# A two-layer sequence model on one core: first weights ahead of the modulations, head decay as one minimum, schedule offsets redone

## The chip, the cores and the metric

The kernel runs on one core of a Trainium2 chip. The metric is device time in microseconds of one execution. Runs of one kernel agree within some 0.1 to 0.3%. Busy times, starts and waits come from one execution under the hardware profiler. Engines are written as in the profile: PE is the matrix engine, PEld its weight loads, DVE the vector engine, ACT the scalar engine, POOL the general engine, SP the queue that issues most DMAs.

## What is computed

Two layers over 256 context tokens and 256 latent tokens of width 1024, all in float32. Every norm is followed by a modulation, whose shift, scale and gate come from a product of SiLU(c) with a 1024 x 6144 matrix for each layer.

```python
for layer in range(DEPTH):                     # DEPTH = 2, ctx_out = layer 0 only
    m_lat = jnp.split(silu_c @ mod_w[layer] + mod_b[layer], 6)      # m_ctx likewise from c_ctx
    h_lat = modulate(rms_norm(lat, norm_mix_g[layer]), m_lat[0], m_lat[1])
    if layer % 2 == 0: y_ctx, y_lat = s5_retention_mixer(h_ctx, h_lat, ...)
    else:              y_ctx, y_lat = mlstm_mixer(h_ctx, h_lat, ...)
    lat = lat + m_lat[2] * y_lat
    h2 = modulate(rms_norm(lat, norm_mlp_g[layer]), m_lat[3], m_lat[4])
    lat = lat + m_lat[5] * (relu(h2 @ mlp_w1[layer]) ** 2 @ mlp_w2[layer])
    ...                                        # the same for ctx in layer 0
return rms_norm(lat, final_norm_g)
```

The even mixer projects the input to `u, q, k, v, g`, runs a bidirectional complex diagonal state space model (S5) on `u` and a bidirectional retention with four heads on `q, k, v`. Retention weighs a score of positions i and j with `exp((i-j) * log_gamma)` in the one direction and `exp((j-i) * log_gamma')` in the other; this factor is what `decay` builds. The odd mixer is an mLSTM.

## The kernel before

The Python code does not issue instructions in the order in which it is written. It records operations in a plan, each with its engine, its tiles and a group name (`u`, `mods`, `norm0`, `nm0`, ...; `.w` marks weight loads, `.s` streamed weights of modulations). A list scheduler (`order`, `run`, `in_order`) then fixes one program for each engine: it takes operations by a rank, with an offset of the rank for each group, and lets a group take new buffers only up to a horizon ahead of the most urgent operation, with an allowance for each group. `SHIFT` holds (offset, allowance) by group, `HORIZON` the horizon, and `AGAIN` further passes with their own tables; the best pass by the scheduler's own costs is taken. `emit` issues everything, so nearly every instruction bears line 745 of the code (746 in the changed kernel). Each engine runs its program in order, and an instruction that waits holds up all that stands behind it on that engine.

Weights come as 128x1024 tiles of 512 KB. Products are done in a split format: ACT casts a tile to its high part (`CAST w<-w`), DVE subtracts to get the low part (`TENSOR_TENSOR w<-w,w`), which is called a split below, and three matmuls (high by high, low by high, high by low) make one product. Activations are split in the same way, unit by unit (eight units `k` of 128 features, 512 tokens or twice 256).

The opening is written as follows. The input x is loaded, its squares are summed, and `rstd_of` makes the root. Eight modulations `mod_first` load 2 x 512 KB of weights each, do eight matmuls with `sc` (SiLU of c, from the small input `cc`) into a row, which ACT copies to `mrow`, and four tiny matmuls with `msel` turn it into columns. `mod_gain` and `norm_k` then give the units of the first norm (`norm0`). The four weight tiles of the first product `u` are loaded after that, then the S5 parameters are computed on DVE (`s5_parameters`, many instructions of 128x64). `plan.behind` names a DMA that all DMAs recorded after it have to follow. `LATE` lists the modulations whose weights go to tiles of the large pool `w` (10 tiles of 128x1024) instead of two halves in the pool `b` (59 tiles of 128x512).

`decay(hd, kt)` builds from the distances `dk` (128x256) the exponent `lg*max(dk,0) + lneg*min(dk,0)` with two TENSOR_SCALARs and an add, and three exponentials. It is called eight times.

Three norms stand between two dense products: `nm0` ahead of the first MLP (around 325 us in the profile), `nm` ahead of the second layer's mixer (around 700), `nm1` ahead of the last MLP (around 982). At each, PE adds up squares (`MATMUL ps<-ones,b`), DVE makes the root in nine tiny instructions on `rs`, PE broadcasts it (`MATMUL ps<-ident,rs`), DVE and ACT make the units, and the MLP's first products take the units with three weight tiles.

Of the kernel before, what the change touches and what calls it, by code (L numbers as in the profile page):

```python
# [21 lines left out]
HORIZON, ROUNDS = 73, 6  # L22
SHIFT = {"": (-41, 76), "chu00": (-8, 8), "chu01": (0, 156), "chu10": (0, -100), "chu11": (0, 27), "decay0": (0, 8),
# [41 lines left out]
)  # L65
MAGIC = 12582912.0
LIGHT = {(0, 0): range(8), (0, 1): (1, 3, 5, 6, 7), (1, 0): (1, 3, 5, 6, 7)}
LATE = (1, 3, 6)
VEC = {}
_off = 0  # L70
for _n, _w in (("modb", 96), ("nmix", 16), ("nmlp", 16), ("nfin", 8), ("bglu", 8), ("retgn", 4),
# [1174 lines left out]
def even_mixer(x):  # L1246
# [321 lines left out]
    def decay(hd, kt):  # L1568
        f, b = hd, 4 + hd
# [337 lines left out]
```

## Time and profile before

| | |
|---|---|
| runs (three) | 1183.42 us median, 1182.99 to 1184.41 |
| profiled execution | 1184.34 us, span 1182.6 us |
| granted PE clock, mean | 0.988 |
| busy in the span | PE 1133.5, PEld 963.2, DVE 832.1, ACT 553.7, POOL 30.5 us |
| DMA | 182.24 MB, mean 154 GB/s |

The span is the time from the first to the last instruction that the profiler saw. Busy time of PE counts matmuls that run one behind the other without a gap as busy. In a timeline row the first number is the start, the second the length of a group of like instructions that follow each other, `x` their count, and what stands in brackets is the engine's idle time just before and the row that ended it. In a row of a stretch (start:end, length) each engine's busy time follows with its number of instructions, then the granted PE clock, the share of the DMA engines and GB/s.

### The profile page before, as it was taken

The numbers are of one execution on the slowest core, as the hardware profiler recorded it, in microseconds if no ns is written. First come the engines' busy times: TensorE is split into PE (matmuls) and PEld (weight loads), VectorE is DVE, ScalarE is ACT, GpSimd is POOL, SyncE is SP. The second block draws the span as 40 slices with busy tenths as digits, with TensorE's granted clock in tenths as the row PEclk, the third lists the DMA queues.
The fourth block names the chain that finished last, engine by engine and source line by source line (L and its number), as shares of the span: only waits on it lengthen the run. The fifth ranks groups of instructions, "written<-read, shape, count | busy, mean of one in ns | idle before, by whom it ended". The sixth has DMA issues, their size and how long they took to land.

```text
span 1182.6 us, 18205 instructions
## 1 busy us (share of the span) xinstructions
PE 1133.5 (96%) x7104; PEld 963.2 (81%) x7104; DVE 832.1 (70%) x1635; ACT 553.7 (47%) x902; POOL 30.5 (3%) x61
## 2 busy tenths in 40 slices
PE   5799999999999999999999999999999998999996
PEld 3577786778998777887878898688788997999996
DVE  7999999658989685347543577669677656763755
ACT  4636656433363422122432346468856544543642
POOL 0000000000001010011000000000000000000000
PEclk9799999999999999999999999999999998999998
DMA  8764645315446375357352523425322353555642
GB/s 309 272 205 141 226 155 181 113 45 175 148 142 176 112 265 195 108 197 264 107 178 71 165 94 95 128 90 161 107 70 57 98 187 121 181 187 189 200 158 90
DMA packets 65750, 182.24 MB, mean 154 GB/s; under 512 B 11136, under 2 KB 17472, under 8 KB 65664
## 3 DMA queue, kind: packets, MB, share of 16 engines
q1 hardware_dynamic: 57600, 151.71, 39.4%
q0 software_dynamic: 8064, 29.36, 7.7%
q8 instruction: 56, 0.92, 0.3%
q14 instruction: 30, 0.25, 0.1%
HBM read 178.20 MB, written 2.85 MB: 153 GB/s over the span
## 4 chain that ended last, share of the span: by engine, by line
PE 72%; DVE 9%; ACT 2%; issue 1%; DMA 1%; DVEq 0%; SPq 0%; ACTq 0%
PE ps L745 72%; DVE b L745 7%; DVE w L745 1%; ACT b L745 1%; DMA b<-in_bdq 1%; DVE rs L745 0%; ACT w L745 0%; ACT L745 0%; DVE mv L745 0%; DVE sm L745 0%; DVE tz L745 0%; DVE e L745 0%; ACT tz L745 0%; DVEq L1903 0%; DVE den L745 0%
## 5 line engine op out<-in xcount | busy, mean ns | idle before, releaser
L745 PE MATMUL ps<-b,w 128*128 128x256 f32 (+1 forms) x5232 | 921.0, 335 | 6.5 <-ACT w L745 2.5
L745 PEld LDWEIGHTS ps<-b,w 128*128 128x128 f32 x5232 | 781.6, 189 | 121.3 <-issue 11.4
L745 DVE TENSOR_TENSOR w<-w,w 128x1024 fp32r<-128x1024 f32 x209 | 255.7, 1224 | 172.0 <-PE ps L745 110.7
L745 ACT CAST w<-w 128x1024 fp32r<-128x1024 f32 x209 | 218.7, 1049 | 319.1 <-PE ps L745 153.2
L745 DVE TENSOR_TENSOR b<-b,b 128x512 f32<-128x512 f32 (+4 forms) x287 | 154.5, 557 | 51.5 <-ACT b L745 45.1
L745 PE MATMUL ps<-b,b 128*128 128x256 f32 (+5 forms) x832 | 142.6, 338 | 4.0 <-ACT b L745 1.8
L745 PEld LDWEIGHTS ps<-b,b 128*128 128x128 f32 (+2 forms) x832 | 97.9, 169 | 31.3 <-issue 17.0
L745 DVE SCALAR_TENSOR_TENSOR e<-e,sc,e 128x1024 f32<-128x1024 f32 x70 | 88.0, 1280 | 7.1 <-DMA e<-in_modc 6.6
L745 ACT ACTIVATE b<-ps 128x256 f32<-128x256 f32 (+1 forms) x112 | 49.9, 459 | 72.5 <-PE ps L745 71.4
L745 ACT COPY b<-ps 128x256 f32<-128x256 f32 (+4 forms) x136 | 60.4, 463 | 37.8 <-PE ps L745 32.3
L745 ACT ACTIVATE b<-b 128x256 f32<-128x256 f32 (+1 forms) x78 | 38.6, 503 | 72.9 <-DVE b L745 65.9
L745 ACT CAST b<-b 128x256 fp32r<-128x256 f32 (+1 forms) x120 | 57.3, 497 | 27.3 <-DVE b L745 26.1
L745 DVE SCALAR_TENSOR_TENSOR b<-b,vec,b 128x512 f32<-128x512 f32 (+1 forms) x80 | 52.7, 694 | 9.4 <-ACT b L745 9.1
L745 DVE TENSOR_TENSOR b<-b 128x256 f32<-128x256 f32 (+2 forms) x95 | 44.1, 479 | 18.2 <-ACT b L745 18.1
L745 DVE SCALAR_TENSOR_TENSOR b<-ps,mc,b 128x256 f32<-128x256 f32 x72 | 32.7, 479 | 26.6 <-PE ps L745 26.3
L745 POOL DMA_DIRECT2D e<-in_modc x56 | 29.7, 531 | 646.3 <-DVE e L745 406.4
L745 ACT ACT_TABLE_LOAD x34 | 43.6, 1283 | 1.5 <-PEq L1899 0.7
L745 PE MATMUL ps<-ones,b 128*128 128x1 f32 x112 | 15.6, 258 | 15.8 <-DVE b L745 14.9
L745 DVE SCALAR_TENSOR_TENSOR b<-ps,b 128x512 f32<-128x512 f32 (+1 forms) x32 | 19.3, 621 | 16.2 <-PE ps L745 10.7
L745 PEld LDWEIGHTS ps<-ones,b 128*128 128x128 f32 x112 | 15.8, 211 | 17.4 <-DVE b L745 15.1
L745 PE MATMUL ps<-w,b 128*128 128x256 f32 x192 | 24.7, 284 | 0.2 <-DVE w L745 0.2
L745 PEld LDWEIGHTS ps<-w,b 128*128 128x128 f32 x192 | 23.4, 188 | 1.6 <-issue 1.0
(114 smaller groups left out, 504.5 us busy)
## 6 DMA issues: line engine op xcount, KB each, us to landing
w<-in_w SPq DMA_DIRECT2D x128, 512.0 KB, 4.3
e<-in_modc POOLq DMA_DIRECT2D x56, 512.0 KB, 4.4
m<-in_modc SPq DMA_DIRECT2D x24, 512.0 KB, 4.7
w<-in_evin SPq DMA_DIRECT2D x16, 512.0 KB, 5.5
w<-in_mlx SPq DMA_DIRECT2D x16, 512.0 KB, 4.5
w<-in_mlo SPq DMA_DIRECT2D x16, 512.0 KB, 3.7
w<-in_mlout SPq DMA_DIRECT2D x16, 512.0 KB, 3.9
b<-in_modw SPq DMA_DIRECT2D x20, 256.0 KB, 5.5
```

The source lines that it names most:

```text
L745: o.ins.append(getattr(engine, name)(*[f(a) for a in args], **{k: f(v) for k, v in kw.items()}))
```

## The change

1. The four weight tiles of `u` are recorded ahead of the modulations, and the modulations' loads from the second pair on (i = 1, 2, 3) have to follow the third of these four loads.
2. `LATE` is empty: all modulation weights of the opening lie in halves in the pool `b`. It is 32 loads of 256 KB now, in place of 20 of 256 KB and 6 of 512 KB.
3. `decay` makes the exponent as `min(lg*dk, lneg*dk)`: an ACT copy with a scale gives `lneg*dk`, and one SCALAR_TENSOR_TENSOR multiplies and takes the minimum.
4. `HORIZON` goes from 73 to 110, many entries of `SHIFT` and all of `AGAIN` are replaced.

```diff
-HORIZON, ROUNDS = 73, 6
+HORIZON, ROUNDS = 110, 6
-         ... "nm": (25, 54), "nm0": (-25, -30), "nm1": (68, -98), "norm0": (-66, 226), ...
+         ... "nm": (0, 227), "nm0": (-25, -30), "nm1": (68, -98), "norm0": (-72, 226), ...
-         (125.3, {"": (3.9, 135), "chu00": (0, 65), ...
+         (42.5, {"": (-9, 130), "chu00": (0, 10), ...
-LATE = (1, 3, 6)
+LATE = ()
@@ even_mixer
         x.ss_add(ss, k)
+    with x.plan.group("u"):
+        w_u = [x.weight(I["evin"][i]) for i in range(4)]
+    hold = [o for o in x.plan.ops if o.dma][-2]
     r = x.rstd_of(ss, 0, 1.0 / 1024)
     h = ([], [])
     for i in range(4):
+        x.plan.behind = hold if i else None
         x.plan.run_in("mods", x.mod_first, 4 + i)
         x.plan.run_in("mods", x.mod_first, i)
         x.mod_gain(0, 0, True, 2 * i, 2)
         for k in (2 * i, 2 * i + 1):
             x.plan.run_in("norm0", x.norm_k, h, r, k, 0, 0)
-    with x.plan.group("u"):
-        w_u = [x.weight(I["evin"][i]) for i in range(4)]
     x.plan.behind = [o for o in x.plan.ops if o.dma][-4]
@@ decay
-        ts(e, dk, 0.0, MAX, lg[:, f:f + 1], MUL)
-        ts(c2, dk, 0.0, MIN, lneg[:, b:b + 1], MUL)
-        tt(e, e, c2, ADD)
+        act(c2, dk, AF.Copy, scale=lneg[:, b:b + 1])
+        stt(e, dk, lg[:, f:f + 1], c2, MUL, MIN)
```

The tables change the order of the whole program. Where the prediction speaks of it, the engines' programs read as follows. In a row stands the line, the operation, the tile written and the tiles read (name, buffer or record numbers) and the shape.

DVE in the opening, before; `vec` holds the S5 constants, `lgs` and the `b` tiles of 128x64 their intermediate values, `sc` is the input of the modulations:

```order
L745 SCALAR_TENSOR_TENSOR lgs_153<-vec_115 128x8
L745 TENSOR_SCALAR b_44_160<-vec_115 128x64
L745 TENSOR_TENSOR b_46_171<-vec_115 128x64
L745 TENSOR_SCALAR b_44_160<-b_44_160 128x64
L745 TENSOR_TENSOR b_46_171<-vec_115 128x64
L745 TENSOR_SCALAR b_44_160<-b_44_160 128x64
L745 TENSOR_TENSOR b_46_171<-b_46_171 128x64
L745 SCALAR_TENSOR_TENSOR b_44_160<-b_44_160 128x64
L745 RECIPROCAL b_46_171<-b_46_171 128x64
L745 SCALAR_TENSOR_TENSOR b_44_160<-b_44_160 128x64
L745 TENSOR_TENSOR sc_81<-sc_81,cc_119 128x8x2
```

In the changed order two pieces of DVE's program, the first with the second and the third of the four splits of `u` (w_58, w_61), the second with the multiplication for `sc`:

```order
L746 SCALAR_TENSOR_TENSOR b_53_213<-b_53_213 128x64
L746 SCALAR_TENSOR_TENSOR rs_52_209<-rs_52_209 128x4
L746 TENSOR_TENSOR w_58_238<-w_39_148,w_56_223 128x1024
L746 SCALAR_TENSOR_TENSOR b_53_213<-b_53_213 128x64 x2
L746 TENSOR_SCALAR b_53_213<-b_53_213 128x64
L746 TENSOR_TENSOR w_61_247<-w_41_153,w_59_240 128x1024
```

```order
L746 SCALAR_TENSOR_TENSOR b_73_300<-b_73_300 128x64
L746 TENSOR_TENSOR b_73_300<-b_73_300 128x64 x2
L746 TENSOR_TENSOR pw_23_111<-b_78_318,b_77_314 128x64
L746 TENSOR_TENSOR b_75_309<-b_75_309,b_44_159 128x64
L746 TENSOR_TENSOR b_73_300<-b_73_300 128x64
L746 TENSOR_TENSOR b_81_331<-pw_23_111 128x128
L746 TENSOR_TENSOR sc_73<-sc_73,cc_215 128x8x2
L746 TENSOR_TENSOR b_77_314<-pw_21_107,pw_23_111 128x64
```

The multiplication that makes `sc` was the 34th row of DVE's program and is the 115th; the splits of `u` and the S5 parameters (down to the powers `pw`) now stand ahead of it.

PE at the norm `nm0`, before, from a modulation (`pick`) on: triples with tiles w_653/w_699 and then w_700/w_704 of the first MLP, one after the other for one unit (b_714, b_718):

```order
L745 MATMUL ps_716_3424<-e_638_2920,pick_87 32x256 x4
L745 MATMUL ps_716_3424<-e_636_2911,pick_87 32x256 x4
L745 MATMUL ps_720_3441<-b_714_3420,w_653_2991 128x256
L745 MATMUL ps_720_3441<-b_714_3420,w_699_3291 128x256
L745 MATMUL ps_720_3441<-b_718_3436,w_653_2991 128x256
L745 MATMUL ps_723_3449<-ones_75,b_678_3124 128x1
L745 MATMUL ps_723_3449<-ones_75,b_702_3319 128x1
L745 MATMUL ps_723_3449<-ones_75,b_678_3124 128x1
L745 MATMUL ps_723_3449<-ones_75,b_702_3319 128x1
L745 MATMUL ps_729_3464<-b_714_3420,w_700_3303 128x256
L745 MATMUL ps_729_3464<-b_714_3420,w_704_3348 128x256
L745 MATMUL ps_729_3464<-b_718_3436,w_700_3303 128x256
```

In the changed order one tile (w_708/w_717) takes all units first:

```order
L746 MATMUL ps_698_3206<-b_681_3075,w_707_3294 128x256
L746 MATMUL ps_672_3037<-ident_401,mrow_678_3062 128x128 x2
L746 MATMUL ps_729_3453<-b_722_3437,w_708_3321 128x256
L746 MATMUL ps_729_3453<-b_722_3437,w_717_3414 128x256
L746 MATMUL ps_729_3453<-b_726_3447,w_708_3321 128x256
L746 MATMUL ps_729_3453<-b_730_3457,w_708_3321 128x256
L746 MATMUL ps_729_3453<-b_730_3457,w_717_3414 128x256
L746 MATMUL ps_729_3453<-b_735_3467,w_708_3321 128x256
L746 MATMUL ps_729_3453<-b_727_3449,w_708_3321 128x256
L746 MATMUL ps_729_3453<-b_727_3449,w_717_3414 128x256
L746 MATMUL ps_729_3453<-b_733_3463,w_708_3321 128x256
L746 MATMUL ps_729_3453<-b_737_3471,w_708_3321 128x256
```

DVE there, before, from the last add ahead of the norm's first product (`gm`) to the second of the tiles' splits (w_722):

```order
L745 TENSOR_TENSOR b_678_3124<-b_678_3124,b_702_3319 128x256
L745 SCALAR_TENSOR_TENSOR b_712_3416<-b_529_2403,gm_522_2373,ps_711_3404 128x256
L745 TENSOR_TENSOR b_713_3418<-b_531_2407,ps_711_3404 128x256
L745 SCALAR_TENSOR_TENSOR b_715_3422<-b_537_2436,gm_522_2373,ps_711_3404 128x256
L745 SCALAR_TENSOR_TENSOR b_547_2471<-ps_690_3198,mc_81_325,b_547_2471 128x256
L745 SCALAR_TENSOR_TENSOR b_718_3436<-b_712_3416,mc_81_325,b_714_3420 128x256
L745 TENSOR_TENSOR b_719_3439<-b_534_2425,ps_711_3404 128x256
L745 TENSOR_TENSOR w_722_3447<-w_705_3350,w_717_3433 128x1024
```

In the changed order, the end of the first stream's units and the two splits that follow (w_751, w_753):

```order
L746 SCALAR_TENSOR_TENSOR b_740_3483<-b_731_3459,mc_123_493,b_734_3465 128x256
L746 TENSOR_TENSOR b_742_3487<-b_732_3461,b_737_3471 128x256
L746 TENSOR_TENSOR b_743_3489<-b_581_2638,ps_719_3420 128x256
L746 SCALAR_TENSOR_TENSOR b_581_2638<-ps_698_3206,mc_123_493,b_581_2638 128x256
L746 TENSOR_TENSOR b_747_3504<-b_739_3478,b_744_3491 128x256
L746 TENSOR_TENSOR b_748_3506<-b_741_3485,b_745_3497 128x256
L746 TENSOR_TENSOR b_689_3143<-b_689_3143,b_711_3356 128x256
L746 TENSOR_TENSOR mc_123_493<-ps_672_3037,vec_119 128x16
L746 TENSOR_TENSOR b_750_3518<-b_746_3502,b_749_3508 128x256
L746 TENSOR_TENSOR w_751_3521<-w_688_3141,w_718_3417 128x1024
L746 TENSOR_TENSOR w_753_3531<-w_673_3046,w_714_3387 128x1024
L746 TENSOR_SCALAR rs_755_3540<-ps_752_3526 128x2
```

The splits stand behind the whole first stream instead of among its first units.

DVE ahead of the norm `nm1`, before; w_1688 and w_1693 are splits of the last MLP's tiles, b_1655 the sum of squares, `rs` the root:

```order
L745 TENSOR_TENSOR w_1684_8991<-w_1669_8862,w_1678_8930 128x1024
L745 TENSOR_TENSOR w_1685_8993<-w_1670_8865,w_1681_8970 128x1024
L745 SCALAR_TENSOR_TENSOR b_1169_6006<-ps_1667_8844,mc_871_4216,b_1169_6006 128x256
L745 TENSOR_TENSOR b_1655_8751<-b_1655_8751,b_1687_9013 128x256
L745 TENSOR_TENSOR w_1688_9034<-w_1676_8925,w_1682_8987 128x1024
L745 SCALAR_TENSOR_TENSOR b_1224_6338<-ps_1674_8907,mc_871_4216,b_1224_6338 128x256
L745 SCALAR_TENSOR_TENSOR b_1224_6338<-ps_1623_8506,mc_871_4216,b_1224_6338 128x256
L745 TENSOR_TENSOR w_1693_9046<-w_1683_8989,w_1689_9036 128x1024
L745 TENSOR_TENSOR b_1655_8751<-b_1655_8751,b_1692_9044 128x256
L745 TENSOR_SCALAR rs_1697_9058<-ps_1696_9053 128x2
```

In the changed order:

```order
L746 TENSOR_TENSOR b_1649_8661<-b_1649_8661,b_1692_9024 128x256
L746 SCALAR_TENSOR_TENSOR b_1222_6317<-ps_1676_8878,mc_961_4833,b_1222_6317 128x256
L746 SCALAR_TENSOR_TENSOR b_1222_6317<-ps_1668_8806,mc_961_4833,b_1222_6317 128x256
L746 TENSOR_TENSOR b_1649_8661<-b_1649_8661,b_1694_9039 128x256
L746 TENSOR_SCALAR rs_1697_9050<-ps_1696_9045 128x2
L746 TENSOR_SCALAR rs_1697_9050<-rs_1697_9050 128x2
L746 TENSOR_TENSOR rs_1697_9050<-rs_1697_9050 128x2 x2
L746 SCALAR_TENSOR_TENSOR rs_1697_9050<-rs_1697_9050 128x2 x2
L746 TENSOR_TENSOR rs_1697_9050<-rs_1697_9050 128x2
L746 SCALAR_TENSOR_TENSOR rs_1697_9050<-rs_1697_9050 128x2 x2
L746 TENSOR_TENSOR w_1699_9063<-w_1678_8896,w_1689_8984 128x1024
L746 SCALAR_TENSOR_TENSOR b_1701_9067<-b_1127_5707,gm_1353_6996,ps_1698_9060 128x256
```

A split (w_1699) stands right behind the root, and the other two (w_1725, w_1729) stand behind nearly all units:

```order
L746 SCALAR_TENSOR_TENSOR b_1720_9113<-b_1715_9100,mc_961_4833,b_1717_9104 128x256
L746 SCALAR_TENSOR_TENSOR b_1722_9120<-b_1716_9102,mc_961_4833,b_1719_9111 128x256
L746 SCALAR_TENSOR_TENSOR b_1723_9122<-b_1718_9109,mc_961_4833,b_1721_9118 128x256
L746 SCALAR_TENSOR_TENSOR b_1724_9127<-b_1222_6317,gm_1353_6996,ps_1698_9060 128x256
L746 TENSOR_TENSOR w_1725_9132<-w_1685_8946,w_1702_9069 128x1024
L746 SCALAR_TENSOR_TENSOR b_1727_9139<-b_1724_9127,mc_961_4833,b_1726_9134 128x256
L746 TENSOR_TENSOR w_1729_9145<-w_1680_8901,w_1700_9065 128x1024
```

No split is left between the last residual products and the sum of squares.

More of the change, by code (lines that the diff above doesn't have):

```diff
@@ L21 @@
 CAPS = {"b": 59, "w": 10, "e": 5, "m": 2, "ps": 8, "mrow": 2, "rs": 3, "tz": 2, "mv": 2, "mv1": 2, "den": 2}
-HORIZON, ROUNDS = 73, 6
-SHIFT = {"": (-41, 76), "chu00": (-8, 8), "chu01": (0, 156), "chu10": (0, -100), "chu11": (0, 27), "decay0": (0, 8),
[18 rows of a table removed]
-AGAIN = (
[5 rows of a table removed]
-         268), "gat1.w": (111.2, 353), "glu": (-3.9, 304), "glu.w": (-20.4, 128), "gt": (-3, 368), "gt.w": (-2.4,
[16 rows of a table removed]
+HORIZON, ROUNDS = 110, 6
+SHIFT = {"": (-41, 76), "chu00": (-8, 8), "chu01": (0, 162), "chu10": (0, -100), "chu11": (0, 27), "decay0": (0, 8),
[19 rows of a table added]
+AGAIN = (
[22 rows of a table added]
 )
```

80 rows, old and new, of tables (AGAIN, SHIFT) are left out of this document.

## Prediction

> **What bounds the kernel now.** I read the page first, then the engines' busy time by stretches, then TensorE's (PE) row of the timeline, where idle time stands in brackets behind the row that ended it, and last VectorE's (DVE) row at the places where PE waits.
>
> ```profile
> span 1182.6 us, 18205 instructions
> PE 1133.5 (96%) x7104; PEld 963.2 (81%) x7104; DVE 832.1 (70%) x1635; ACT 553.7 (47%) x902; POOL 30.5 (3%) x61
> PE 72%; DVE 9%; ACT 2%; issue 1%; DMA 1%; DVEq 0%; SPq 0%; ACTq 0%
> ```
>
> The span is 1182.6 us in an execution of 1184.34, which is 0.92 above the median of 1183.42. PE is busy for 96%, so over the whole there are some 49 us to lose or win; the 9% of DVE in the chain that ended last shows who holds them. The stretches say where:
>
> ```profile
> core 0: us, PE busy (x) PEld busy (x) DVE busy (x) ACT busy (x) POOL busy (x), PEclk, DMA share, GB/s
> 30.00:50.00 20.00, 13.04 (x101) 8.48 (x94) 20.00 (x84) 12.03 (x26) 0.00 (x0) 0.70 1.01 390
> 50.00:72.00 22.00, 21.47 (x88) 16.65 (x87) 22.00 (x56) 10.95 (x18) 0.00 (x0) 0.96 0.15 42
> 12.00:220.00 208.00, 192.08 (x1383) 144.41 (x1384) 201.97 (x541) 115.44 (x220) 1.21 (x2) 0.97 0.62 209
> 220.00:250.00 30.00, 30.00 (x215) 24.24 (x214) 13.57 (x38) 10.14 (x19) 0.53 (x1) 1.00 0.25 76
> 345.00:600.00 255.00, 254.78 (x1144) 204.15 (x1143) 159.66 (x184) 80.63 (x105) 21.10 (x40) 1.00 0.55 181
> 705.00:930.00 225.00, 221.65 (x1246) 184.51 (x1246) 163.80 (x372) 147.87 (x247) 0.00 (x0) 1.00 0.33 98
> ```
>
> From 12 to 220 us DVE is busy 202.0 of 208 us: there DVE is the bound, and PE has 15.9 us of idle time. From 220 us on PE is the bound (30.00 of 30, 254.78 of 255), but for short stops where a norm stands between two products. So a DVE instruction that is saved or pushed back counts in the first stretch, later only at those stops, and whatever PE loses is not won back after 220 us. Rows of PE, DVE and the DMA issues in the opening:
>
> ```profile
> 16.18 1.94 PE L745 MATMUL ps<-b,sc 128*32 128x256 f32 x16 [0.19 <-DVE lgs L745]
> 41.47 1.01 PE L745 MATMUL ps<-msel,mrow 128*128 128x2 f32 x4 [4.16 <-ACT mrow L745]
> 46.24 10.62 PE L745 MATMUL ps<-b,w 128*128 128x512 f32 x34
> 57.39 2.97 PE L745 MATMUL ps<-b,w 128*128 128x512 f32 x11 [0.53 <-DVE w L745]
> 12.35 0.19 DVE L745 TENSOR_SCALAR b<-vec 128x64 f32<-128x64 f32 x1
> 13.76 0.16 DVE L745 TENSOR_TENSOR sc<-sc,cc 128x16 f32<-128x16 f32 x1
> 21.65 3.08 DVE L745 TENSOR_TENSOR b<-b,ps 128x512 f32<-128x512 f32 x5
> 17.36 7.48 SPq L745 DMA_DIRECT2D b<-in_modw  x12
> 33.61 0.33 SPq L745 DMA_DIRECT2D w<-in_modw  x1
> ```
>
> The first modulation runs at 16.18 us, the last one late (its row is waited for until 41.47), the first product `u` starts at 46.24. The transfers' issues run at 7.48/12 = 0.62 us for each 256 KB.
>
> **The decays.** Each of eight drops two TENSOR_SCALARs and one TENSOR_TENSOR of 128x256 for one SCALAR_TENSOR_TENSOR, and one ACT copy comes in.
>
> ```profile
> L745 DVE TENSOR_SCALAR b<-b,lgs 128x256 f32<-128x256 f32 x16 | 5.1, 350 | 0.0
> L745 DVE TENSOR_TENSOR b<-b,b 128x256 f32<-128x256 f32 x62 | 26.0, 422 | 16.9 <-ACT b L745 16.5
> L745 DVE SCALAR_TENSOR_TENSOR b<-b,vec,b 128x256 f32<-128x256 f32 x16 | 7.1, 478 | 0.0
> L745 ACT COPY b<-ps 128x256 f32<-128x256 f32 x56 | 19.7, 374 | 7.1 <-PE ps L745 5.0 <-DVE b L745 2.0
> ```
>
> Neighbours on DVE overlap by about 0.08 us, so back to back these are 0.26, 0.34 and 0.39 us: 2 x 0.26 + 0.34 - 0.39 = 0.47 us of DVE, 3.7 for eight. The 16 TENSOR_SCALARs' 5.1 busy us are the union of the rows, so no more than 16 x 0.35 could be gained there. ACT gets 8 x 0.37 = 3.0 us, in a stretch where it is busy 115 of 208: nothing, except that each copy stands in the chain of its decay.
>
> **The opening.** The first product's four weights now come before most modulations. On the DMA queue 54 units of 256 KB (47 before) stand ahead of the last modulation's weights, with the input of the modulations (`cc`) itself moved from row 10 to row 22: 7 x 0.62 = 4.3 us later. On DVE the four splits (1.13 us each, from 328.30 to 329.43 in the rows further down) and nearly all of the S5 parameters stand ahead of the multiplication that makes `sc`, which ran at 13.76; by the rows' durations that is 16.5 us of work from 12.35 on, so PE's first modulation goes from 16.2 to about 29, and 16 of them follow at 1.0 to 1.9 us per 16 matmuls, with the last weights landing 4 to 5 us later than now. The norm's products on DVE, which began at 21.65, move to 39. I get the start of `u` at 48.5 to 49 instead of 46.24. Then `u` has all four tiles ready, but its third unit of the input comes from DVE only at about 60, since eight products of the S5 tables stand ahead of it; `u` ends at about 77.7 instead of 72.2, with 1.45 us of other matmuls pulled in. PE is then 4.0 us behind.
>
> How much of this is left at 250 us hangs on DVE, the bound. I add up DVE's durations in program order up to each place where PE takes from it, and the PE work that is left from there. The largest of these sums is 1134.6 before (second pair of heads) and 1138.5 in the changed order (the S5 outputs and first heads, at 188 us): 3.9 more, though the decays' 3.7 is in it, because more table and weight work is ahead of that place. The distance between such a sum and the real clock, DVE's waits and the gaps between its instructions, grows with time (7.8 us at 200, 9.9 at 218); the new maximum lies 30 us earlier, so it has 2 to 3 us less of it. 3.9 - 2.8 = **+1.1 us**; bounds: -3.7, if only the decays' saving arrives, and +4.0, if the whole delay of `u` stays.
>
> **The norm before the first MLP.** Rows of PE and DVE there, with the broadcast of the root at T = 325.41:
>
> ```profile
> 325.41 0.61 PE L745 MATMUL ps<-ident,rs 128*128 128x128 f32 x4
> 325.77 1.31 PE L745 MATMUL ps<-b,w 128*128 128x256 f32 x9
> 327.01 1.07 PE L745 MATMUL ps<-e,pick 128*32 128x256 f32 x16
> 329.29 4.60 PE L745 MATMUL ps<-b,w 128*128 128x256 f32 x36
> 326.06 0.48 DVE L745 SCALAR_TENSOR_TENSOR b<-b,gm,ps 128x256 f32<-128x256 f32 x1 [0.77 <-PE ps L745]
> 326.45 0.41 DVE L745 TENSOR_TENSOR b<-b,ps 128x256 f32<-128x256 f32 x1
> 326.78 0.47 DVE L745 SCALAR_TENSOR_TENSOR b<-b,gm,ps 128x256 f32<-128x256 f32 x1
> 328.30 1.22 DVE L745 TENSOR_TENSOR w<-w,w 128x1024 fp32r<-128x1024 f32 x1
> 329.43 0.47 DVE L745 SCALAR_TENSOR_TENSOR b<-b,mc,b 128x256 fp32r<-128x256 f32 x1
> ```
>
> Now PE takes three weight tiles in turn for each unit of the norm's output (36 matmuls in 4.43 us, 0.37 for three), so a unit gives it 1.1 us of work and DVE keeps up; it loses 0.4 us. In the changed order one tile is split ahead of the norm, the other two only behind all 18 norm instructions of the first stream. DVE starts them at T+0.65: 7 at 0.39 and 11 at 0.335 make 6.5 us, the last unit is there at T+7.2, the two splits at T+8.3 and T+9.4. PE has until then 1.9 us of other matmuls and eight triples of 0.37, ending at T+7.6: idle 7.6 - 1.9 - 2.95 = 2.75 us, less the 0.4 of now: **+2.4**. Bounds 0 (if ACT and DVE deliver so that PE is filled) and +4.5.
>
> **The last norm.**
>
> ```profile
> 975.79 3.47 PE L745 MATMUL ps<-b,w 128*128 128x256 f32 x28
> 981.77 1.05 PE L745 MATMUL ps<-ones,b 128*128 128x1 f32 x8 [2.52 <-DVE b L745]
> 984.65 1.22 PE L745 MATMUL ps<-ident,rs 128*128 128x128 f32 x4 [1.82 <-DVE rs L745]
> 986.99 12.15 PE L745 MATMUL ps<-b,w 128*128 128x256 f32 x87 [1.11 <-ACT b L745]
> 980.16 1.22 DVE L745 TENSOR_TENSOR w<-w,w 128x1024 fp32r<-128x1024 f32 x1
> 985.91 1.26 DVE L745 SCALAR_TENSOR_TENSOR b<-b,gm,ps 128x256 f32<-128x256 f32 x3 [1.32 <-PE ps L745]
> 980.00:984.00 4.00, 1.05 (x8) 0.97 (x8) 2.68 (x9) 1.75 (x3) 0.00 (x0) 0.94 0.82 266
> 987.00:990.00 3.00, 3.00 (x13) 2.86 (x14) 3.00 (x9) 1.94 (x5) 0.00 (x0) 0.50 0.00 0
> ```
>
> Here the split at 980.16 stands ahead of the add that the sums (981.77) wait for. In the changed order the three splits are behind the root: one right ahead of the norm's products, under the broadcast's wait (1.32 us idle before 985.91), two behind nearly all of them. The sums come 1.4 us earlier. Then DVE has 15 instructions of 0.39 from T+1.26 (T = the broadcast), the second tile's split ends at T+8.3, and 17 triples of 0.355 are left: T+14.3. Before, the 24 triples are done at T+12.7 (987 to 999.1 less 15 matmuls of another tile). +1.6 - 1.4 = +0.2, and the clock, half between 984 and 990 now, stays low some 1.2 us' worth longer since PE runs thin until T+8.3; half of that is mine: **+0.8**, bounds -1.4 and +4.
>
> The clock at the first MLP's norm I leave at full: PE is busy half of the time there, against 1.05 of 4.00 us in the row 980 to 984, after which it was 0.50. Should it fall, 3.4 us of dense matmuls run at half speed, +1.7. The Trainium skill (TensorE: Matmul & The Clock Gate, What's actually happening) lets the clock drop only after an idle window of about 3.4 us; by it nothing falls at either norm. This trace differs: the longest wait at the last norm is 2.52 us and the clock still halved, so the idle share decides here, not one long gap.
>
> The other norm (odd layer, some 3 us lost now) has less work under it but two splits right behind the first unit: 0, within 1 us. Between 705 and 930, where PE idles 3.4 us by the row and small waits of several kinds follow each other, the order is new everywhere, and I have no sign: 0, within 2.
>
> **Sum.** 1.1 + 2.4 + 0.8 = +4.3 on 1184.34 gives 1188.6 for such an execution, **1187.7** against the median.
>
> **Rivals.** *Faster:* the DVE-bound stretch shortens. It has 6.0 us of DVE idle and the 3.7 of the decays; if the early splits fill 3 of the 6 (the first product waited 0.53 us for a split at 57.39), the stretch gives -6.7, and with +3.2 at the norms the time is 1179.9. It decides from -5.6 us at 220 on (3.2 and the 2.4 that can be told from no change). For it: 202 of 208 us. Against: the larger sum at 188 us, and the first product that waits in a new place. *No change:* the decays' 3.7 arrive in full and the norms take back 3.2: 1182.9. *Slower still:* the whole 4.0 of the opening remains and the clock falls at the first MLP's norm: 4.0 + 2.4 + 1.7 + 0.8 = 8.9, 1192.3.
>
> **Numbers.** A measurement here tells 0.2%, 2.4 us. Forecast with its upper rival: 0.56 (0.42 for 1186 to 1190, 0.14 above); no change 0.20; faster 0.24. The range from 1178 to 1194 leaves out a tenth or less at either end; the forecast alone would be 1185.8 to 1190.
>
> **What would show it.** `u` should start at 48 to 49.5 and end near 77.5; PE's idle time up to 250 us should be about 1 us more than now, with DVE still busy over 95%; around 330 us PE should show seven or eight stops of 0.3 to 0.5 us with DVE as releaser; the sums of the last norm should follow the last product within 1.5 us instead of 2.5. I am wrong if `u` ends before 74, or if DVE's idle time in the opening falls by more than 2 us.

## The result and the profile after

The changed kernel takes 1204.58 us (median of four, 1203.33 to 1207.52); the kernel before took 1183.91 beside it. The ratio is 1.0183, 95% interval 1.0170 to 1.0196: about 21 us slower, where 1187.7 was forecast and the range ended at 1194. The page's head and its chain of the changed kernel:

```profile
span 1203.4 us, 18195 instructions
PE 1136.7 (94%) x7104; PEld 963.8 (80%) x7104; DVE 829.1 (69%) x1619; ACT 560.6 (47%) x912; POOL 30.4 (3%) x61
PE 71%; DVE 16%; DMA 5%; ACT 4%; issue 3%; SPq 0%; POOL 0%; DVEq 0%; ACTq 0%; POOLq 0%
```

PE does the same 7104 matmuls in nearly the same busy time, and DVE is busy 3.0 us less. Nearly all of the loss is waiting (PE's busy time grows by 3.2 us, the span by 20.8): in the chain that ended last DVE goes from 9% to 16% and DMA from 1% to 5%. Five of the six stretches that stood in the prediction, now:

```profile
30.00:50.00 20.00, 16.22 (x169) 9.94 (x169) 20.00 (x89) 9.56 (x22) 0.00 (x0) 0.84 1.00 330
50.00:72.00 22.00, 20.21 (x87) 15.49 (x88) 22.00 (x42) 11.84 (x24) 0.00 (x0) 0.83 0.30 105
12.00:220.00 208.00, 177.72 (x1409) 135.05 (x1409) 194.12 (x507) 114.10 (x222) 1.06 (x2) 0.96 0.57 189
220.00:250.00 30.00, 30.00 (x137) 24.11 (x135) 28.98 (x40) 13.77 (x22) 3.69 (x7) 1.00 0.77 269
705.00:930.00 225.00, 217.41 (x1208) 177.21 (x1208) 174.74 (x396) 152.82 (x247) 3.70 (x7) 0.99 0.37 119
```

From 12 to 220 us PE loses 14.4 us against before (177.72 for 192.08), and DVE is not fuller but emptier: 194.12 busy for 201.97. From 705 to 930 PE loses 4.2. PE's row in the opening:

```profile
30.31 6.06 PE L746 MATMUL ps<-b,sc 128*32 128x256 f32 x80 [13.56 <-DVE sc L746]
49.98 7.64 PE L746 MATMUL ps<-b,w 128*128 128x512 f32 x24
60.41 0.80 PE L746 MATMUL ps<-ident,b 128*128 128x128 f32 x4 [1.79 <-DVE b L746]
60.86 18.47 PE L746 MATMUL ps<-b,w 128*128 128x512 f32 x72
```

The modulations wait 13.56 us for `sc` and run from 30.31, `u` starts at 49.98 and ends at 79.2 (72.2 before). One execution is not exact here: in the profiles of e3 and h1 (below), which run the program of the kernel before up to this place, `u` starts at 43.21 and 44.51 instead of 46.24.

To place the loss I matched the two traces matmul by matmul and took, at the same amount of PE work done, start time plus PE work still to come. How much later the changed kernel stands against the kernel before, worked out from one profile of each; beside it the same for two kernels of the experiments:

| PE work done, us | place | after: starts at, behind by | g4 behind by | g6 behind by |
|---|---|---|---|---|
| 30 | end of `u` | 75, 5.7 | 1.4 | 3.6 |
| 60 | S5 tables | 107, 4.6 | 1.4 | 2.3 |
| 80 | S5 tables | 132, 9.4 | 1.4 | 6.8 |
| 160 | heads | 227, 13.5 | 1.7 | 10.7 |
| 260 | output projection | 329, 13.0 | 1.8 | 10.0 |
| 300 | behind `nm0` | 372, 15.8 | 1.7 | 12.9 |
| 620 | end of the first MLP | 693, 14.5 | 1.8 | 11.6 |
| 740 | odd mixer | 827, 21.8 | 2.9 | 17.1 |
| 900 | ahead of `nm1` | 996, 21.6 | 2.8 | 16.9 |
| 1060 | last MLP | 1163, 21.3 | 4.0 | 16.6 |

Four pieces: `u` (5.7 here), some 7 us from there to the output projection (5.7 to 13.0), 2.8 at `nm0`, 7 in the odd mixer; the stretches between take back about 2.

The piece at `u` scatters with PE's granted clock. In the eight profiles with this opening (after, g5, g6, g8 to g12) it is 2.6 to 5.9, on the mean 4.1: 2.6 to 2.8 where the clock of 50 to 72 us is 0.94 to 0.96 (g5, g8, g9), 3.6 to 5.1 where it is 0.91 to 0.87 (g6, g10, g12), 5.7 and 5.9 where it is 0.83 and 0.84 (after, g11).

The rows at 107, 132 and 227 us don't place the second piece more closely, since the two orders take matmuls of different kinds first there. PE's idle time by stretches does so roughly. Before:

```profile
72.00:120.00 48.00, 46.75 (x379) 36.45 (x379) 46.35 (x84) 26.13 (x51) 0.00 (x0) 1.00 0.63 202
120.00:190.00 70.00, 67.35 (x581) 53.13 (x580) 68.91 (x160) 42.50 (x84) 0.68 (x1) 1.00 0.61 202
190.00:220.00 30.00, 27.90 (x147) 19.16 (x147) 28.37 (x73) 17.73 (x35) 0.54 (x1) 1.00 0.47 150
```

and after:

```profile
72.00:120.00 48.00, 44.85 (x373) 36.39 (x372) 42.16 (x82) 26.95 (x51) 0.00 (x0) 1.00 0.64 191
120.00:190.00 70.00, 66.47 (x556) 50.91 (x555) 64.96 (x139) 41.49 (x85) 0.53 (x1) 1.00 0.42 136
190.00:220.00 30.00, 26.39 (x215) 18.82 (x213) 27.14 (x56) 18.11 (x36) 0.53 (x1) 0.94 0.46 162
```

PE is idle 1.9 us more from 72 to 120 us, 0.9 more from 120 to 190 and 1.5 more from 190 to 220, where a clock of 0.94 costs another 1.8 (0.06 x 30).

### The profile page after: what moved, and what is told of

Same layout as the page of the kernel before. It is cut to its first block, busy times and chain, and to the rows that moved or that the text cites. A ratio compares the mean times of both kernels' runs of the same rounds, so it can differ in the third digit from the quotient of the medians.

```text
span 1203.4 us, 18195 instructions
## 1 busy us (share of the span) xinstructions
PE 1136.7 (94%) x7104; PEld 963.8 (80%) x7104; DVE 829.1 (69%) x1619; ACT 560.6 (47%) x912; POOL 30.4 (3%) x61
## 4 chain that ended last, share of the span: by engine, by line
PE 71%; DVE 16%; DMA 5%; ACT 4%; issue 3%; SPq 0%; POOL 0%; DVEq 0%; ACTq 0%; POOLq 0%
PE ps L746 71%; DVE b L746 12%; ACT b L746 3%; DVE w L746 2%; DMA w<-in_mlx 1%; DMA dram<-b 1%; DVE e L746 1%; ACT L746 1%; DMA e<-in_modc 1%; DMA b<-in_xT 1%; DVE rs L746 0%; DMA b<-in_modw 0%; DMA m<-in_modc 0%; DVE mv L746 0%; ACT w L746 0%
## 5 line engine op out<-in xcount | busy, mean ns | idle before, releaser
L746 DVE TENSOR_TENSOR b<-b,b 128x512 f32<-128x512 f32 (+4 forms) x287 | 152.0, 556 | 64.8 <-ACT b L746 61.2
L746 DVE TENSOR_TENSOR b<-b 128x256 f32<-128x256 f32 (+2 forms) x87 | 40.8, 483 | 13.8 <-ACT b L746 13.8
L746 DVE TENSOR_TENSOR b<-pw,b 128x512 f32<-128x512 f32 x36 | 23.7, 689 | 2.1 <-DMA dram<-b 2.0
```

The costliest lines, as they stand in the source:

```text
L746: o.ins.append(getattr(engine, name)(*[f(a) for a in args], **{k: f(v) for k, v in kw.items()}))
```

## Experiments

Names in the expectations: a number behind a letter is another experiment of this list. From f on, the scheduler is replaced by a written list of all operations and one of all buffers:

```diff
-        best = self.order(HORIZON, ROUNDS)
-        self.slot, self.n = best[3], 0
+        self.slot, self.n = {b: s for b, s in zip(self.bufs, SLOTS) if s >= 0}, 0
...
-                self.emit(best[2])
+                self.emit(ORDER)
```

### The parts of the change: e1, e2, e3

e1 is the kernel after with the offsets of the kernel before, e2 the reverse.

```diff
-HORIZON, ROUNDS = 110, 6      # e1; SHIFT and AGAIN of before as well
+HORIZON, ROUNDS = 73, 6
```

> The changed code (first weights early, all modulation weights in small buffers, new decay) under the old tables of offsets, allowances and horizon, so that only the order differs from the changed kernel. Theory A (order: DVE's work ahead of the places where PE takes from it, plus DVE's waits, sets the time at 250 us, and the new tables are what made the waits long): the sum of DVE durations and PE work left is 1139.0 us at most here, the waits come out between those of before (7.5 us at 188) and of the changed kernel (14.9), so 5 to 8 us over before in the opening and little elsewhere: 1186 to 1194 us. Rival B (the structure costs: weights of u ahead of the modulations delay every order): as slow as the changed kernel, 1200 to 1208. Rival C (structure free, tables all of it): 1180 to 1186.

> The code of before under the new tables. Theory A: the sum of DVE durations and PE work left reaches 1164 us (at the retention's values, 175 us of DVE work ahead), 29 more than before; with 8 to 15 us of DVE waits the time is 1205 to 1225. Rival B (the structure costs, tables do not): 1181 to 1190.

Measured: 1272.09 (ratio 1.0750, 1.0734 to 1.0766) and 1277.08 (1.0779, 1.0754 to 1.0804). No theory had this. A table of offsets seems to fit only the recorded program that it was made for (why, no run shows); the two halves can't be priced apart in this way.

e3 is the kernel before, in its own order, with the new decay at the place of the old one:

```diff
-V tensor_scalar, V tensor_scalar, V tensor_tensor
+A activation (copy with scale), V scalar_tensor_tensor
```

> The order of before, instruction by instruction, with each decay's two TENSOR_SCALARs and add replaced where they stood by an ACT copy with a scale and one SCALAR_TENSOR_TENSOR with a minimum. It measures the decay alone. Theory A (DVE is the bound to 220 us): 0.47 us of DVE saved eight times, of which that ahead of the deciding place counts: 1180 to 1182, -2 to -3.7 us. Rival (the copies lengthen the chains through ACT, or PE hides it): 1183 to 1185.

Measured: 1183.37, ratio 0.9999 (0.9989 to 1.0008). The stretch 120 to 220 us in the kernel before (behind the length PE, PEld, DVE busy):

```profile
120.00:220.00 100.00, 95.25 (x727) 72.29 (x726) 97.28 (x231) 60.23 (x119) 1.21 (x2) 1.00 0.57 187
```

and in e3:

```profile
120.00:220.00 100.00, 94.93 (x717) 71.11 (x715) 93.53 (x214) 62.20 (x124) 1.21 (x2) 1.00 0.56 183
```

DVE is relieved of 3.75 us, as was worked out, in a stretch where it was busy 97%; PE's time does not move. The saved time came back as waiting. This was the first sign that a busy DVE is not the bound.

### Order and buffers: f1 to f4, g4

f1 takes the order of before up to the last matmul of `u` and the order of after from there, f2 the reverse, f3 the order of after to some 280 us and then that of before. f4 runs the changed operations throughout in the order of before.

> The changed code with a fixed order: up to the last matmul of the first product u, the instructions stand in the order of the kernel before (its late first weights included); all the rest stands in the order of the changed kernel. Theory A (the losses of the changed order lie in several places that add up; PE's start of u is one of them, 5.5 us): 1197 to 1200 us. Rival B (the late u is what makes the later waits of DVE, on the write of u's result to memory and after, so that the opening carries most of the 13 us lost by 250 us): 1190 to 1195. Rival C (DVE's throughput absorbs the opening): 1203 to 1206.

> The mirror image: the changed kernel's order up to the last matmul of u, the order of the kernel before from there on. Theory A: 1183.6 + 5.5 = 1189. Rival B (u's delay makes later waits): 1192 to 1197. Rival C (absorbed by 250 us): 1183 to 1185.

> The changed kernel's order up to the first output product of the even mixer (about 280 us), the order of before from there on. Theory A: the opening's 12.9 us stay, the later losses (first MLP's norm +3, odd layer +8, last norm and gate 0) go: 1195 to 1198. Rival (the later losses come with the early part's transfers and buffers, not with the later order): 1202 to 1206.

> The changed code (small buffers for all modulation weights, new decay) with every instruction at the place it had before; the weights of u are loaded where they were. Theory A (structure costs nothing, the order is all): 1182 to 1185. Rival (loads into small buffers or the ACT copies cost): 1187 or more.

Measured: f1 1213.87 (1.0262), f2 1210.48 (1.0230), f3 1197.78 (1.0120, 1.0103 to 1.0136), f4 1193.07 (1.0082, 1.0059 to 1.0104). f1 and f2 are slower than either parent: behind the seam many buffers had to take other places (in f1 DVE waits 4.4 us at 85.8 for a buffer that is still being written to DRAM, and 2.9 at 92.4 for PE), so neither answers what was asked. f3, in theory A's range, puts some 14 of the 21 us ahead of 280 us, roughly, since it has a seam too; the table's 13.0 at 260 agrees. f4 came out some 10 us above the kernel before (1183.15 beside it), and 273 of its 2038 buffers lay elsewhere than there; g4 repeats it with every old buffer at its old place.

> The kernel after, its instructions in the order of the kernel before (each instruction at the place that its counterpart has there, the added splits at the place of the load they follow), and every buffer that has a counterpart in the kernel before in that counterpart's slot; only the modulation weights' halves, which are new in the small buffers, take free slots. f4 had the same order, but 273 of 2038 buffers in other slots, and took 1193.07. Theory A (the 20 us of the kernel after come from the order and the choice of buffers, not from what the change computes or loads): 1181 to 1186, ratio 0.998 to 1.002, with the first product's matmuls some 2 us earlier than in the kernel before and the DVE stretch of 12 to 220 us at 198 to 202 us busy. Then the choice of slots alone cost f4 7 to 12 us. Theory B (weights in small buffers cost by themselves, through the pool that they fill): 1190 to 1196, as f4.

Measured: 1185.29, ratio 1.0019 (1.0006 to 1.0032): theory A. The 2 us by which `u` was to be earlier did not come; in the profile, which is the slowest of g4's eight runs (1188.09), it stands 1.4 later. DVE's waits from 12 to 220 us in f4 that g4 has not (sum, times, longest):

```profile
DVE w L959 <- ACT w L959: 3.8, 1, 3.8
DVE w L959 <- issue: 2.1, 1, 2.1
```

These two rows, 5.9 us for tiles of the pool `w`, are gone in g4.

So the changed operations, small buffers and new decay included, cost 2 us (1 to 4) when they run in the old order, and the choice of buffers alone, in the same order, is worth 7.8 us (1193.07 to 1185.29). All but some 2 of the 21 us are the new order with the buffers that go with it.

### The odd mixer: g6

> The kernel after with two weight tiles of the odd layer staged in the two modulation buffers of the same size, which stand empty from early on, and their loads put on SyncE's queue where it blocked: issued near 712 us instead of 735.6. All ten weight slots are held there until 735 to 738 us, and five loads then land together at 743.0 to 750.3; ScalarE waits 3.36 us for one and 1.88 us for another with activations queued behind that PE needs. Theory A (the 8 us lost at 705 to 785 us come from weights that are late because their slots are held): 1199.5 to 1202.7, the casts' waits for loads gone or under 1 us, and the loss of 705 to 785 us at 3 to 6 us. Theory B (the stretch is held by ScalarE's and VectorE's own order, the late loads are hidden): 1203.5 to 1206. Theory C (the earlier loads delay the third gate tile's, which lands at 717.45): 1206 to 1209.

```diff
-2 tiles: pool w (10 tiles, all held), DMA behind 711.31 on SP: issued from 735.62 on
+2 tiles: pool m (2 tiles, empty here), DMA at the same place on SP
```

SP's row in the kernel after, with the stop:

```profile
711.31 0.48 SPq L746 DMA_DIRECT2D b<-in_bdv  x1
735.62 0.33 SPq L746 DMA_DIRECT2D w<-in_mlx  x1
```

ACT's row there, with the casts that wait for the tiles:

```profile
743.05 1.05 ACT L746 CAST w<-w 128x1024 fp32r<-128x1024 f32 x1 [3.36 <-DMA w<-in_mlx]
747.93 1.05 ACT L746 CAST w<-w 128x1024 fp32r<-128x1024 f32 x1 [1.88 <-DMA w<-in_mlx]
```

ACT's wait for such loads in 705 to 790 us is 3.36 + 1.88 = 5.2 us. In g6, by the view of waits:

```profile
ACT w L961 <- DMA w<-in_mlx: 0.2, 1, 0.2
```

and SP's row of g6, with the two loads into the pool `m`:

```profile
708.88 0.90 SPq L961 DMA_DIRECT2D m<-in_mlx  x2
```

Measured: 1200.25, ratio 1.0144 (1.0127 to 1.0161), 4.3 us less than after. The loads go out some 26 us earlier and ACT's wait for them falls from 5.2 to 0.2 us. The same repair made 3.6 us between g9 and g10 and 1.6 between g11 and g12 (below; g12 scatters from 1199.95 to 1206.62, so this one alone is not clear of noise). The traces give less: in the table the stretch from 693 to 996 us loses 7.1 us in the kernel after and 5.3 in g6, and the rest of g6's lead stands ahead of 693, where the edit does nothing. Matched in the same way, the five profiles without the repair (after, g5, g8, g9, g11) lose 6.0 to 8.8 us there and the three with it (g6, g10, g12) 3.8 to 6.4, which is 2.5 less on the mean. Theory A holds, for some 2 to 3 us, about a third of what is lost in this stretch.

### Single waits of the opening: g5, g8, g9, g11

g5 takes away VectorE's two longest waits behind `u`, for buffers whose contents are still being written to DRAM:

```diff
 SP near 72 us
-load val0.w, load val0.w, load qk0.w, write u, write u
+write u, write u, load val0.w, load val0.w, load qk0.w
```

> The kernel after with only SyncE's order changed near 72 us: the writes of two results of the first product to DRAM stand ahead of the three weight loads that were issued before them (at 71.5 to 72.8 us), and another pair of writes ahead of a read. In the trace of the kernel after VectorE waits 1.95 us at 80.91 and 1.81 us at 88.27 for buffers that those writes hold. Theory A (in the opening the end is set by what VectorE loses to such waits): 1200.8 to 1202.7, with the two waits gone and the loss at 120 us smaller by 2 to 3.8 us. Theory B (the wait moves to the next row of the same chain, as the time saved in e3 did): 1203.5 to 1206, no change that can be told. Theory C (the weights that come later then hold up the split and PE): 1206 to 1210.

The two rows of DVE in the kernel after:

```profile
80.91 0.69 DVE L746 TENSOR_TENSOR b<-pw,b 128x512 f32<-128x512 f32 x1 [1.95 <-DMA dram<-b]
88.27 1.42 DVE L746 TENSOR_TENSOR b<-b,b 128x512 f32<-128x512 f32 x2 [1.81 <-DMA dram<-b]
```

In g5 DVE's waits of 60 to 130 us have no row for such a write any more, and a new one:

```profile
DVE w L959 <- ACT w L959: 1.2, 1, 1.2
```

Measured: 1204.24 (1.0182, 1.0165 to 1.0198). 3.8 us of waiting are gone, 2.2 of other waits have come (1.2 in this row), and nothing that can be told is gained: theory B. The 3.8 is one execution's: in g6, whose order is that of the kernel after here, the two waits are 1.2 us in sum.

g8 moves three rows of DVE that PE waits for:

```diff
 DVE near 118 us
+split qk0.w, split val0.w, sum of qk0
 8 sums of chunks and tables
-split qk0.w, split val0.w
 13 rows, most of them sums of tables
-sum of qk0
```

> The kernel after with three instructions of VectorE put some 5 to 14 us earlier, behind the first query-key tile's last product near 118 us: the splits of the second query-key tile (it ran at 123.41) and of a value tile (124.66), and the sum that frees the PSUM buffer of the first query-key tile (132.70); ScalarE's casts of these two tiles change places (102.49 and 117.65), and two weight slots with them. In the trace of the kernel after TensorE waits 4.7 us at 100 to 135 us, 1.7 of it for these splits and casts, 0.6 for the sum, and 2.4 for ScalarE's copies of a table, which this edit leaves. Theory A (TensorE is short of weights there, VectorE has room): 1201.5 to 1203.5, with the waits for splits at 117 to 134 us gone. Theory B (the table instructions that now run 2.9 us later on VectorE hold TensorE up instead, so that the order on VectorE from 113 to 133 us sets the pace): 1204 to 1207.5. What either leaves of the 10 us that the kernel after loses between 80 and 250 us is then not one wait but the whole order.

Measured: 1205.68 (1.0191, 1.0177 to 1.0205). Nothing is gained: theory B. PE's waits for the splits are gone, and its waits at 100 to 135 us fall from 4.7 to 3.5 us. What is left is ACT's copy of a table, which the edit did not touch, and 1.2 us for DVE where it was 0.6 (the longest waits of PE there in g8):

```profile
PE ps L959 <- ACT b L959: 2.0, 1, 2.0
PE ps L959 <- DVE b L959: 1.2, 1, 1.2
```

g9 and g11 go for PE's wait at 202.75, for an S5 table that is read back from DRAM into a buffer of the pool `e`:

```diff
-tab11 -> e1 (in use until 198.6); mod05.s -> e0 (loaded at 144.8, used from 222)
+tab11 -> e0; mod05.s -> e1, loaded behind it
 SP: g9
 load mod04.s, load mod04.s, load mod04.s, load mod04.s, write tab11, read tab11
 SP: g11
 load mod04.s, load mod04.s, write tab11, read tab11, load mod04.s, load mod04.s
```

> The kernel after with one table of the mixer read back from DRAM into another of the five e buffers: into the one that a modulation weight tile holds unused from 144.8 to 222 us (that tile is loaded near 199 us instead, into the other). In the trace of the kernel after the table's read can be issued only at 198.58, when the last use of its buffer ends, and lands at 202.70; TensorE waits 3.46 us for it, with a head's product, another weight's products and the modulations queued behind, and its clock stands at 0.91 and 0.75 in the two 5 us stretches that follow. The table's last sum and the sum of that head on VectorE are also put ahead of the rows they stood behind (from 194.36 to near 188, and from 204.62 to near 197), so that the next row doesn't take the wait over. Theory A (this held buffer is what the 7.0 us of loss near 200 us come from, 2.9 of which the kernel before loses too): 1198 to 1201, with TensorE's wait for the table and for the head's sum gone and the clock at 1.00 there. Theory B (as in e3, g5 and g8, the next row waits instead): 1203 to 1206.

> The repairs of g6 (two weight tiles of the odd layer in other buffers) and g9 (the table's read in another buffer) together, all else as in the kernel after. Theory A (two held buffers at two places, each paid for by itself): the sum of what the two gain alone, 1194 to 1197. Theory B (only the odd layer's is real): 1199 to 1202, as g6. What is then left to the kernel before is the opening up to 135 us (some 10 us) and the first layer's end.

> As g9, with the table's write and read on SyncE ahead of the next two modulation tiles' loads instead of behind them. In g9's trace the write was issued at 193.44, behind loads issued at 191.59 and 192.01, took 4.6 us, and the read landed at 202.25, no earlier than in the kernel after (202.70): TensorE waited 6.3 us for it, and the edit had taken nothing away. Here the write should be issued near 185 to 188 us and the read land before 196. Theory A (the table's late read costs what is lost near 200 us): TensorE's wait for it gone, the clock in 195 to 210 us at 1.00, 1198 to 1201. Theory B (the next row waits instead): 1203 to 1206.

> g6 and g11 together, all else as in the kernel after. g10 joined g6 to g9, whose edit had not taken the wait away, and took 1203.85, 3.6 less than g9. Theory A (two held buffers at two places, each paid for by itself): the sum of the two gains, 1194 to 1197. Theory B (only the odd layer's is real): 1199 to 1202, as g6.

Measured: g9 1207.48 (1.0214), g10 1203.85 (1.0183), g11 1204.95 (1.0178, 1.0164 to 1.0192), g12 1203.39 (1.0164, 1.0143 to 1.0184). PE's longest wait at 180 to 250 us in the kernel after:

```profile
PE ps L746 <- DMA e<-dram: 3.5, 1, 3.5
```

in g9:

```profile
PE ps L959 <- DMA e<-dram: 6.3, 1, 6.3
```

and in g11:

```profile
PE ps L959 <- DVE b L959: 3.9, 1, 3.9
```

g9's edit missed its aim: the write stood behind two more loads in SP's order, the table came as late as before, and the kernel took some 3 us more than the kernel after, beyond both theories' ranges. In g11 the table lands at 196.8 and PE does its products with it from 198.92 on. Then it waits 3.9 us for the operand of the next products, a chunk's sums on DVE, which end at 203.40. In the kernel after they end at 203.50, so PE could not have gone on much earlier there: the wait for the table had hidden all but 0.16 us of the wait for DVE.

```profile
203.56 0.44 PE L746 MATMUL ps<-b,b 128*64 128x128 f32 x4 [0.16 <-DVE b L746]
```

g11 is theory B. g10 and g12 lie above theory B's range and far from theory A's: near 200 us nothing is gained, and what they have over g9 and g11 fits the odd layer's repair.

### What DVE's time is worth: h1, h2

```diff
         for i in order:
             o = self.ops[i]
+            if i in SKIP:     # 16 DVE instructions of chunks, 0.69 us each
+                continue
```

> The kernel before, every instruction and buffer at its place, with 16 VectorE instructions of the mixer's chunks left out: in half of the complex products that make the output weights the second product and the sum (16 times 0.69, 11.1 us by the trace; they run between 50 and 185 us). That part of the mixer is therefore not computed. Theory A (what the prediction went by: VectorE's sum of durations sets the end of 12 to 220 us): 1172 to 1177. Theory B (VectorE's time is covered, the rows wait for one another through three engines; e3 took 3.75 us away and gained nothing): 1180.5 to 1184.

> The kernel after with the same 16 instructions left out, all else at its place (11.0 us by its trace, between 52 and 203 us; the last four stand right ahead of the product that TensorE waits for at 205 us in g11). That part of the mixer is not computed. Theory A (VectorE sets the pace of the opening in this order): 1193.5 to 1198. Theory B (covered, as in the kernel before): 1201 to 1205. If the kernel after gains much more than the kernel before, its order has tied TensorE to VectorE's rows where that of before had TensorE work in hand.

Measured: h1 1181.25, ratio to before 0.998 (0.997 to 0.999), 2.4 us for 11.1 us of DVE work; h2 1201.08, ratio to before 1.0138 (1.0117 to 1.0158), 3.5 us less than the median of after (5 by the two ratios) for 11.0. That is theory B in both. The stretch 12 to 220 us in h1:

```profile
12.00:220.00 208.00, 195.68 (x1422) 147.34 (x1424) 195.41 (x534) 115.48 (x221) 1.21 (x2) 0.95 0.62 210
```

and in h2:

```profile
12.00:220.00 208.00, 183.52 (x1430) 139.77 (x1431) 189.64 (x500) 118.71 (x230) 1.77 (x4) 0.96 0.57 191
```

DVE is busy 6.6 and 4.5 us less there; the rest of what was removed has been filled with rows that moved up. A fifth of the removed time arrives at the end of the kernel before and a third to a half in the kernel after, where PE has more idle time to lose. DVE's sum of durations sets the end of the opening in neither. The stretch behind `u` in the kernel before shows what the old order did well:

```profile
72.00:250.00 178.00, 172.00 (x1317) 132.98 (x1317) 157.20 (x350) 96.50 (x188) 1.74 (x3) 1.00 0.53 172
```

and in the kernel after:

```profile
72.00:250.00 178.00, 167.71 (x1276) 130.24 (x1274) 163.24 (x314) 100.31 (x192) 4.75 (x9) 0.99 0.54 178
```

PE was busy 96.6% there (172.00 of 178.00), DVE 88%, and 97% of the 100 us up to 220. PE's 6.0 us of idle time are all that a relief of DVE behind `u` could have won in the kernel before, so theory A's 6 to 11 us for h1 asked for all of it or more; 2.4 came. The new order leaves PE 4.3 us more idle in this stretch.

## Why the prediction was wrong

- **The opening up to the end of `u`: right.** First modulation about 29 (30.31), `u` from 48.5 to 49 (49.98) to about 77.7 (79.2), PE 4.0 us behind (5.7 in this profile, 4.1 on the mean of eight).
- **What is left of it at 250 us: wrong, and this step failed the prediction.** It was to be +1.1, from "there DVE is the bound": DVE's sum up to PE's rows, plus a distance between sum and clock that I took over from the kernel before (7.8 at 200 us) and even shortened by 2.8. In the changed kernel that distance is twice as large, 14.9 us at 188 us where it was 7.5 (as read for the expectation of e1), and DVE's idle time of 12 to 220 us is 13.9 for 6.0. New waits on DVE were given no price, as if an engine that is busy 97% couldn't get any. PE was 13.0 us behind at the next place that the table tells well (329 us), not 1. And the premise itself does not hold: 3.75 us (e3) and 11.1 us (h1) of DVE work taken out of that stretch gained nothing and 2.4. PE, busy 96.6% behind `u`, had only 6.0 us to win there, which the sum of DVE's durations did not show.
- **The decays: right on DVE, wrong in worth.** 3.7 us saved forecast, 3.75 found; in the sum they counted in full, and measured alone they are worth 0 within 0.1%.
- **`nm0`: right.** +2.4 forecast, +2.8 in the table above (260 to 300); the clock stayed at 1.00, in part by chance: in g5, with the same order here, it was 0.83 over 340 to 350 us, and the same matching gives 3.4. PE's stops are there with the releasers DVE and ACT, though they are fewer than the "seven or eight" and sum to 1.0 us; the rest is matmuls that follow each other more slowly (13 in 2.53 us in the last row, 36 in 4.60 before):

```profile
340.68 0.61 PE L746 MATMUL ps<-ident,rs 128*128 128x128 f32 x4
343.59 0.50 PE L746 MATMUL ps<-b,w 128*128 128x256 f32 x2 [0.23 <-ACT b L746]
344.43 0.97 PE L746 MATMUL ps<-b,w 128*128 128x256 f32 x6 [0.34 <-DVE b L746]
345.82 2.53 PE L746 MATMUL ps<-b,w 128*128 128x256 f32 x13 [0.42 <-DVE b L746]
```

and the stretch, with PE's clock at 1.00:

```profile
340.00:350.00 10.00, 8.83 (x63) 7.52 (x62) 9.71 (x24) 7.29 (x16) 0.00 (x0) 1.00 0.33 111
```

- **`nm1`: right within a microsecond.** +0.8 forecast, about -0.3 found (21.6 to 21.3). The sums wait 0.91 us instead of 2.52, as worked out, and the rest takes it back. The +0.6 for the clock is not found: it stays at half to 1013 us in this profile, and in g6, where it is at 1.00 again from 1006.5 on, 2 us sooner after the broadcast, the table has the same -0.3 (16.9 to 16.6). PE's rows in the kernel after:

```profile
1001.70 1.05 PE L746 MATMUL ps<-ones,b 128*128 128x1 f32 x8 [0.91 <-DVE b L746]
1004.58 1.22 PE L746 MATMUL ps<-ident,rs 128*128 128x128 f32 x4 [1.83 <-DVE rs L746]
```

and the stretch behind them, at half the clock as before:

```profile
1004.00:1010.00 6.00, 4.07 (x15) 3.48 (x16) 5.75 (x15) 2.20 (x6) 0.00 (x0) 0.50 0.03 14
```

- **The odd layer: the term was mis-sized.** "0, within 2" for an order that is new everywhere; it lost 7 us between the first MLP and the odd mixer's middle, of which 2 to 3 are two weight tiles that waited for held buffers (g6); the rest is not traced to rows. The order of SP with the pool's occupancy, which would have shown SP stopped behind ten held tiles, was not followed there.
- **The rivals.** None had the size: the slowest ended at 1192.3. All three priced the places where an instruction was seen to move, and none the buffers.

What is shown: the loss is order and buffers, not the operations (g4); buffers alone can cost 7.8 us in a fixed order (f4, g4); held weight buffers cost 2 to 3 us in the odd mixer (g6). What stays open: which rows of the new order make the some 7 us between `u` and the output projection, and the 4 to 5 us left in the odd mixer. Three single waits there were taken away and the next one took their place each time (g5, g8, g11), which fits an order in which many rows are late together, but no run isolates them.

## What to carry to other kernels

An engine's busy share does not make it the bound: take some of its work out and see whether the end moves before a sum is built on it. When a schedule is redone, follow each pool's held buffers and the queue that stops behind them, since a wait that is new has no row in the trace of before. And before a wait is removed, look up when the other operands of the same and the next instructions come: the view of waits names only the last one.

## What the hardware showed

The 64 KB write of the table took 2.5 us in the kernel after (194.68 to 197.18) and 4.6 us in g9, where two loads of 512 KB had been issued 1.4 to 1.9 us ahead of it on the same queue (4.3 in g11, again behind two). At `nm1` the clock stood at 0.50 from 1003 us on, when PE's longest wait there had been 0.91 us and it had been busy for 1.84 of the 3.00 us from 1000 on, part of it with eight matmuls of a single column (128x1); the waits of 1.83 and 1.11 us came behind that. By the Trainium skill (TensorE: Matmul & The Clock Gate, What's actually happening) the clock goes down after an idle window of about 3.4 us. This trace has no such wait ahead of the fall; whether a window with such small matmuls counts as idle is not shown. At `nm0`, with PE busy 8.83 of 10 us, the clock stayed at 1.00 in the kernel after and was 0.83 in g5, where PE was busy 9.24. So these rows don't show either that the idle share alone decides, as the prediction put it.
